# Strassen products in eight of the 22 blocks of an up projection, with their activation sums formed during the output projection

## The chip, the cores and the metric

The kernel runs on one core of one Trainium2 chip. The metric is the device time of an execution in microseconds (us), taken from launch to end on that core. The engines are named as in the profile: PE (matmul) and PEld (its weight load), DVE, ACT, POOL, and SP, which issues the DMAs.

## The reference

Two layers of an encoder trunk on 512 tokens with 1024 features, in float32. In each layer an input projection feeds three branches (latent attention, grouped-query attention, mean pooling), which are gated, merged and sent through an output projection. Then comes the gated feed-forward block, which is where the change lies:

```python
x = x + merged @ w_out[l]
hf = rms_norm(x, ffn_norm_g[l])
u = depthwise_conv(hf @ ffn_w_up[l], ffn_conv_w[l], ffn_conv_b[l])   # 1024 -> 2 * 2816, width 3
u_gate, u_val = u[..., :D_FF], u[..., D_FF:]
x = x + (jax.nn.silu(u_gate) * u_val) @ ffn_w_down[l]                # 2816 -> 1024
```

## The kernel before

**Layout.** Features lie on the 128 partitions and tokens along the free axis. `XM` holds the residual stream as 8 tiles of 128x512. `HH` and `HL` hold the same, scaled by the norm's gains, split in two: a rounded part (high) and the rest (low), both in the fp32r type that PE multiplies. The norm's factor for each token (`rbc`) is applied only when a product leaves PSUM. Every float32 product is three fp32r matmuls: high by high, high by low, low by high (`mm3`, L477, which calls `mm`; all its matmuls show as L470).

**Weights.** They come as a stream of pieces in the order of use. SP loads two pieces at a time into one of three `raw` buffers (`w_dma`). `w_split` (L377) turns a piece of 128x512 into a high part `wh` on ACT and a low part `wl` on POOL, or on DVE where the planner finds it sooner free. `wnext` keeps a few pieces ready ahead of PE.

**Up projection.** The 22 blocks of 128 gate features and the 22 of values are made in two halves, blocks 0 to 11 and 12 to 21 (`HALVES`). A block `c` has part 0 (gate) and part 1 (value). Each part is one PSUM bank filled by 24 matmuls of 512 columns (`feat_major`, L696: 8 tiles of features by three). `up_evac` (L1732) then empties the bank: DVE multiplies by `rbc`, ACT applies the middle tap and the bias, DVE adds the other two taps, ACT takes the silu of the gate, and DVE multiplies gate and value. For an odd block DVE also forms the sums of activations that the down projection wants, in a PSUM bank `q`.

**Down projection.** It already goes by Strassen's scheme. A piece holds a 2x2 group of 128x128 weight blocks, and the activations of a pair of blocks, cut in two halves of 256 tokens, are the other 2x2 group. `products` (L1807) makes seven products instead of eight, each of three matmuls of 256 columns (L1832), into four banks. `w_seven` (L400) prepares the seven left factors: three are blocks of the piece and four are sums. So a piece costs more work beside PE: ACT copies one block into a PSUM bank (`mi` or `S`, in turn), DVE forms the sums there in three instructions of 256, 128 and 128 columns, ACT writes their high part, DVE their low part (128x512), and the plain blocks are split as before (128x384). `unite` (L1836) adds the four banks to two tiles of `XM` on DVE, with the last two additions on POOL. Six PSUM banks (`acc`, `ST`, `AV`, two each) serve the up and the down projection.

**What sets the order.** All engines run what was written for them, in order. The program decides that order while it is built: a planner (`Clock`) keeps an imagined time with a cost for each instruction, and `chain` writes an instruction when its predecessors are done on that imagined time. The planner has no part in the execution; only the order that it wrote is left.

## Time and profile before

| | |
|---|---|
| median of 3 runs | 1551.59 us (1550.44 to 1551.61) |
| the profiled execution | 1551.91 us, of it 1550.1 us of span |
| granted clock | 0.999 |
| PE busy, matmuls | 1531.9 us, 7760 |
| PEld, DVE, ACT, POOL busy | 1307.6, 1090.8, 870.7, 1031.7 us |
| DMA | 166.63 MB, 107 GB/s |

The stages of the feed-forward block, read from PE's instructions by their tiles:

| stage | layer 0, us | layer 1, us |
|---|---|---|
| output projection | 379.0 to 422.8 | 1147.6 to 1191.4 |
| up, blocks 0 to 11 (and part 0 of 12) | 422.8 to 559.0 | 1191.4 to 1327.5 |
| down, first half | 559.0 to 621.3 | 1327.5 to 1389.9 |
| up, rest | 621.3 to 724.7 | 1389.9 to 1493.3 |
| down, second half | 724.7 to 776.0 | 1493.3 to 1544.6 |

A matmul's own duration in the trace overlaps with the next one's, so PE's cost is read from the starts: time of a stretch divided by the matmuls in it. A row of a view that groups instructions names line, engine, operation, tiles written and read, shape and count, then busy time, mean duration in ns, and the idle time before with what ended it.

### The profile page before, as it was taken

Reading aid. Unit: us, or ns where it says so; the run is one execution under the profiler, and the core shown is the slowest. Engines: PE = TensorE matmul, PEld = TensorE weight load, DVE = VectorE, ACT = ScalarE, POOL = GpSimd, SP = SyncE. Lnnn points to the kernel's source line nnn. Section 1 sums busy time; section 2 is a strip of 40 time slices with the busy share of each in tenths; the row PEclk is TensorE's granted clock in tenths of the full one; section 3 lists DMA queues with packets and bytes.
Section 4 is the critical chain, followed back from the end, with each engine's and each line's share of the span. In section 5 each row is a group of like instructions: output and inputs, shape, how many; then the busy total and the mean of one; then the engine's idle time right before and its main releaser. Section 6 shows DMA issues by size and latency. Waiting matters only on the chain.

```text
span 1550.1 us, 22862 instructions
## 1 busy us (share of the span) xinstructions
PE 1531.9 (99%) x7760; PEld 1307.6 (84%) x7760; DVE 1090.8 (70%) x1986; ACT 870.7 (56%) x1695; POOL 1031.7 (67%) x983
## 2 busy tenths in 40 slices
PE   9999999999999999999999999999999999999998
PEld 8888788788888889888988877888888888998888
DVE  6778889986255576557956788899762655765586
ACT  6557786663444455445644587776634455544453
POOL 4965986854666645665789659878547666465654
PEclk9999999999999999999999999999999999999999
DMA  6432234434333333333445322444243233233223
GB/s 217 114 113 77 75 102 133 124 91 141 104 95 97 95 91 106 106 98 91 132 126 138 105 70 75 117 139 125 82 147 99 96 96 95 90 116 96 95 90 101
DMA packets 82725, 166.63 MB, mean 107 GB/s; under 512 B 20912, under 2 KB 42672, under 8 KB 82608
## 3 DMA queue, kind: packets, MB, share of 16 engines
q1 hardware_dynamic: 82464, 165.16, 34.7%
q8 instruction: 61, 1.00, 0.3%
q14 instruction: 56, 0.46, 0.1%
q10 hardware_dynamic: 144, 0.01, 0.0%
HBM read 151.50 MB, written 13.63 MB: 107 GB/s over the span
## 4 chain that ended last, share of the span: by engine, by line
PE 87%; DVE 5%; ACT 3%; POOL 3%; issue 1%; DVEq 0%; POOLq 0%; ACTq 0%
PE ps_acc L470 34%; PE ps_AV L470 19%; PE ps_ST L470 15%; PE ps_AV L1832 5%; PE ps_ST L1832 5%; PE ps_acc L1832 4%; PE ps_S L470 2%; PE ps_mi L470 2%; PE ps_ST L1430 1%; POOL qa L272 1%; DVE XM L272 1%; ACT ps_ST L264 1%; DVE mgl L272 1%; POOL oraw L272 0%; ACT wh L264 0%
## 5 line engine op out<-in xcount | busy, mean ns | idle before, releaser
L272 POOL TENSOR_TENSOR wl<-raw,wh 128x512 fp32r<-128x512 f32 (+3 forms) x498 | 608.6, 1229 | 403.6 <-ACT wh L264 378.2
L264 ACT ACTIVATE wh<-raw 128x512 fp32r<-128x512 f32 (+2 forms) x521 | 300.9, 590 | 31.4 <-DMA raw<-w 12.0
L470 PE MATMUL ps_acc<-HH,wh 128*128 128x512 f32 x608 | 237.2, 390 | 0.2
L470 PE MATMUL ps_acc<-HL,wh 128*128 128x512 f32 x608 | 236.9, 390 | 0.0
L470 PE MATMUL ps_acc<-HH,wl 128*128 128x512 f32 x608 | 236.8, 389 | 0.0
L470 PEld LDWEIGHTS ps_acc<-HH,wh 128*128 128x128 f32 x608 | 114.2, 188 | 24.2 <-issue 0.8
L470 PEld LDWEIGHTS ps_acc<-HH,wl 128*128 128x128 f32 x608 | 114.2, 188 | 24.0
L470 PEld LDWEIGHTS ps_acc<-HL,wh 128*128 128x128 f32 x608 | 114.2, 188 | 23.2
L470 PE MATMUL ps_AV<-HH,wh 128*128 128x512 f32 x288 | 112.4, 390 | 0.0
L470 PE MATMUL ps_AV<-HL,wh 128*128 128x512 f32 x288 | 112.1, 389 | 0.0
L470 PE MATMUL ps_AV<-HH,wl 128*128 128x512 f32 x288 | 112.1, 389 | 0.0
L470 PE MATMUL ps_ST<-HH,wh 128*128 128x512 f32 x224 | 87.3, 390 | 0.0
L470 PE MATMUL ps_ST<-HL,wh 128*128 128x512 f32 x224 | 87.2, 389 | 0.0
L470 PE MATMUL ps_ST<-HH,wl 128*128 128x512 f32 x224 | 87.1, 389 | 0.0
L470 PEld LDWEIGHTS ps_AV<-HH,wl 128*128 128x128 f32 x288 | 54.1, 188 | 11.4
L470 PEld LDWEIGHTS ps_AV<-HH,wh 128*128 128x128 f32 x288 | 54.1, 188 | 11.0
L470 PEld LDWEIGHTS ps_AV<-HL,wh 128*128 128x128 f32 x288 | 54.1, 188 | 10.9
L276 DVE SCALAR_TENSOR_TENSOR a<-ps_acc,prm,a 128x511 f32<-128x511 f32 x64 | 47.9, 748 | 21.4 <-ACT a L264 20.5
L1832 PE MATMUL ps_ST<-ah,wh 128*128 128x256 f32 x278 | 55.5, 284 | 2.3 <-ACT wh L264 2.3
L276 DVE SCALAR_TENSOR_TENSOR a<-ps_AV,prm,a 128x511 f32<-128x511 f32 x56 | 42.0, 749 | 21.3 <-ACT a L264 20.3
L276 DVE SCALAR_TENSOR_TENSOR a<-ps_ST,prm,a 128x511 f32<-128x511 f32 x56 | 41.9, 749 | 20.0 <-ACT a L264 19.2
L264 ACT ACTIVATE gt<-gt 128x512 f32<-128x512 f32 x48 | 30.2, 628 | 45.3 <-DVE gt L272 45.1
(479 smaller groups left out, 4328.9 us busy)
## 6 DMA issues: line engine op xcount, KB each, us to landing
raw<-w SPq DMA_DIRECT2D x228, 512.0 KB, 3.5
raw<-w SPq DMA_DIRECT2D x13, 384.0 KB, 3.1
XM<-x SPq DMA_DIRECT2D x16, 256.0 KB, 3.4
dtq<-tr SPq DMA_DIRECT2D x16, 192.0 KB, 1.9
dtk<-tr SPq DMA_DIRECT2D x16, 192.0 KB, 2.0
tf<-dtq SPq DMA_DIRECT2D x48, 64.0 KB, 2.1
tf<-dtk SPq DMA_DIRECT2D x48, 64.0 KB, 2.1
raw<-w SPq DMA_DIRECT2D x6, 448.0 KB, 3.4
```

The lines of the kernel that those rows point to most:

```text
L264: return self.eng.activation(out, in_, func, **k)
L272: return self.eng.tensor_tensor(out, *a)
L276: return self.eng.scalar_tensor_tensor(out, *a)
L470: PE.matmul(o, lhsT=lhsT, rhs=rhs, start=start, stop=stop)
L1430: PE.matmul(sc, lhsT=s[a_][:, kb_], rhs=s[b_][:, :T], start=False, stop=n == len(pairs) - 1, skip_group_check=True)
L1832: PE.matmul(o, lhsT=x_, rhs=y_, start=first and b not in seen and q == 0, stop=False, skip_group_check=True)
```

## The change

1. **Blocks 2, 4, 6, 8, 10, 16, 18 and 20** of the up projection are made by `both`: the piece is a 2x2 group of weight blocks (two tiles of features by gate and value of block `c`), and `products` makes seven products for each of the four pairs of feature tiles. 96 matmuls of 512 columns become 84 of 256 columns for each pair of parts. Their 32 pieces per layer go through `w_seven` instead of `w_split`.
2. **The other factor**, the sums of activations (`turned`, tiles `tf`), is formed by `turn_pair` during the output projection, as soon as two tiles of `XM` are complete, in the banks `mi` and `S`; a copy goes to DRAM (`tsp`). The second half loads it back at block 13 (`load_turned`) and splits it again on ACT and POOL, since its 16 tiles are freed between.
3. **Four banks come out of such a block.** DVE adds them to two (five instructions), and those go through `up_evac`.
4. **`products`** takes the plain weight blocks first (2, 1, 4), then the sums' high parts, then their low parts; the old order stays for the pieces marked `late`.
5. **`unite`** puts its last addition on DVE instead of POOL. The very last `unite` has an order of its own with two additions on POOL and one copy on ACT.
6. **Smaller**: banks are taken from whichever tag is free soonest (`bank`) instead of in turn; the bank `q` is taken only when the product is written; the splits of block 11 go to POOL instead of DVE; the second norm of a layer leaves out `tokens` (two DVE instructions) and starts 0.8 after its sum instead of 2.0 in planner time; the first banks of layer 1 are chosen by `bank`.

```diff
+UP_SEVEN = (2, 4, 6, 8, 10, 16, 18, 20)
-    r = [(c, part) for c in range(c0, c1) for part in range(2)]
+    r = [z for c in range(c0, c1) for z in (((c, BOTH),) if c in UP_SEVEN else ((c, 0), (c, 1)))]
...
+        def turn_pair(k):
...
+            return [([("H", G2, k), ("H", G2, k + 1)], begin),
+                    stt(1, lo_, x1, hi_, g1, 0, lo_, ALU.subtract), stt(1, hi_, x2, hi_, g2, 1, lo_, ALU.add), hi(0),
+                    stt(0, lo_, x2, hi_, g2, 0, hi_, ALU.add), stt(0, hi_, x2, lo_, g2, 1, hi_, ALU.subtract), hi(1),
+                    lo(0), keep(0), lambda: free("S"), lo(1), keep(1), lambda: free("mi")]
...
-                eng = V if c + 1 in (HALVES[0][1], HALVES[1][1]) else G
+                eng = V if c + 1 == FC else G
...
-            for n in (2, 1, 3, 6, 5, 4, 7):
+            work = [(n, q) for n in ((2, 1, 3, 6, 5, 4, 7) if late else (2, 1, 4)) for q in range(3)]
+            if not late:
+                work += [(n, q) for n in (3, 6, 5, 7) for q in range(2)] + [(n, 2) for n in (3, 6, 5, 7)]
...
+        def both(c, half):
+            banks_ = {}
+            for k in range(0, KC, 2):
+                t = turned[k]
+                need(("H", G2, k), ("H", G2, k + 1))
+                products(((HH[:, k, :256], HL[:, k, :256]), (HH[:, k + 1, :], HL[:, k + 1, :]), t[:2], t[2:], ("H", G2, k),
+                          ("H", G2, k + 1), ("turned", l, half, k, 0), ("turned", l, half, k, 1)), banks_, k == 0)
...
+            chain(lambda: A.activation(u[:, :256], b1[:, :256], AF.Copy), after=0.0)
+            chain(add(u[:, hi_], u[:, :256], b1[:, hi_]), lambda: free(t1),
+                  add(v[:, :256], u[:, hi_], b3[:, :256]), lambda: free(t3),
+                  add(u[:, hi_], u[:, hi_], b2[:, hi_]), add(b0, u[:, :T], b0), lambda: up_evac(c, 0, b0, t0),
+                  add(pair(b2), bc(v[:, None, :256], [P, 2, 256]), pair(b2)), lambda: up_evac(c, 1, b2, t2), after=0.0)
...
-                  lambda: e.tensor_tensor(pair(x1), pair(x1), u3[:, None, :].to_broadcast([P, 2, 256]), ALU.add),
+                  lambda: V.tensor_tensor(pair(x1), pair(x1), u3[:, None, :].to_broadcast([P, 2, 256]), ALU.add),
```

**What moves on PE.** The first rows are those of block 2 in layer 0 before: HH and HL are the activations, wh and wl the weights' parts, ps_ST a bank.

```order
L470 MATMUL ps_ST_4911<-HH,wh_4843 128x512
L470 MATMUL ps_ST_4911<-HL,wh_4843 128x512
L470 MATMUL ps_ST_4911<-HH,wl_4844 128x512
L470 MATMUL ps_ST_4911<-HH,wh_4843 128x512
L470 MATMUL ps_ST_4911<-HL,wh_4843 128x512
```

The same place in the changed kernel is the end of the first seven products of block 2; wh_0 and wl_0 are the plain blocks of the piece, wh_1 and wl_1 the sums, tf the activation sums.

```order
L1895 MATMUL ps_acc_4927<-tf_4417,wl_0_4816 128x256
L1895 MATMUL ps_acc_4916<-HH,wh_1_4815 128x256
L1895 MATMUL ps_acc_4916<-HL,wh_1_4815 128x256
L1895 MATMUL ps_ST_4921<-tf_4415,wh_1_4815 128x256
L1895 MATMUL ps_ST_4921<-tf_4416,wh_1_4815 128x256
L1895 MATMUL ps_acc_4927<-tf_4415,wh_1_4815 128x256
L1895 MATMUL ps_acc_4927<-tf_4416,wh_1_4815 128x256
L1895 MATMUL ps_AV_4941<-tf_4417,wh_1_4815 128x256
L1895 MATMUL ps_AV_4941<-tf_4418,wh_1_4815 128x256
L1895 MATMUL ps_acc_4916<-HH,wl_1_4817 128x256
L1895 MATMUL ps_ST_4921<-tf_4415,wl_1_4817 128x256
```

One bank filled by matmuls of 512 columns has become four that are filled in turn by matmuls of 256; the low part of the sums (wl_1) is the last thing that a piece needs.

**What moves on DVE in the up projection.** Before, in layer 0 at blocks 3 and 4, DVE only empties banks (rbc, the two taps on a) and forms the sums of activations (t, sMQ).

```order
L272 TENSOR_TENSOR ps_AV_4956<-ps_AV_4956,rbc_4709 128x512
L276 SCALAR_TENSOR_TENSOR a_4996<-ps_AV_4956,prm_88,a_4996 128x511 x2
L272 TENSOR_TENSOR ps_acc_4997<-a_4996,a_4955 128x512
L272 TENSOR_TENSOR t_739_4998<-ps_acc_4997,t_739_4998 128x256
L272 TENSOR_TENSOR t_740_4999<-ps_acc_4997,a_4910 128x256
L272 TENSOR_TENSOR t_740_4999<-ps_acc_4997,t_739_4998 128x256
L272 TENSOR_TENSOR sMQ_4632<-ps_acc_4997,sMQ_4633 128x512
L272 TENSOR_TENSOR ps_ST_5002<-ps_ST_5002,rbc_4709 128x512
L276 SCALAR_TENSOR_TENSOR a_5051<-ps_ST_5002,prm_88,a_5051 128x511 x2
```

In the changed kernel this is where block 2 ends on DVE: u adds up the four banks, and ps_S with raw is the first weight piece of block 4.

```order
L276 TENSOR_TENSOR u_766_5061<-u_766_5061,ps_ST_4921 128x256
L276 TENSOR_TENSOR u_767_5062<-u_766_5061,ps_AV_4941 128x256
L276 TENSOR_TENSOR ps_S_4852<-ps_S_4852,raw_4975 128x256
L276 TENSOR_TENSOR u_766_5061<-u_766_5061,ps_acc_4927 128x256
L276 TENSOR_TENSOR ps_S_4852<-raw_4975,ps_S_4852 128x128
L276 TENSOR_TENSOR ps_acc_4916<-u_766_5061,ps_acc_4916 128x512
L276 TENSOR_TENSOR ps_S_4852<-raw_4975,ps_S_4852 128x128
L276 TENSOR_TENSOR ps_acc_4927<-u_767_5062,ps_acc_4927 128x512
L276 TENSOR_TENSOR ps_acc_4916<-ps_acc_4916,rbc_4784 128x512
L276 TENSOR_TENSOR wl_1_5069<-ps_S_4852,wh_1_5067 128x512
```

Ahead of the emptying of a bank stand now five additions and the four instructions of a weight piece, written in turn; the first addition waits for PE's last product of the block, and all rows behind it wait with it.

**What moves on DVE in the output projection.** Before, each tile of XM gets its residual and its low part, one after the other.

```order
L276 SCALAR_TENSOR_TENSOR XM<-ps_AV_4386,XM 128x512
L276 SCALAR_TENSOR_TENSOR HL<-XM,prm_88,HH 128x512
L276 SCALAR_TENSOR_TENSOR XM<-ps_acc_4427,XM 128x512
L276 SCALAR_TENSOR_TENSOR HL<-XM,prm_88,HH 128x512
L276 SCALAR_TENSOR_TENSOR XM<-ps_ST_4468,XM 128x512
```

Now the sums of tiles 0 and 1 stand between them: four instructions of 256 columns in the banks S and mi, and two low parts tf.

```order
L280 SCALAR_TENSOR_TENSOR ps_S_4420<-XM,prm_89,ps_mi_4419 128x256
L280 SCALAR_TENSOR_TENSOR ps_S_4420<-XM,prm_89,ps_S_4420 128x256
L280 SCALAR_TENSOR_TENSOR ps_mi_4419<-XM,prm_89,ps_mi_4419 128x256
L280 SCALAR_TENSOR_TENSOR XM<-ps_AV_4387,XM 128x512
L280 SCALAR_TENSOR_TENSOR ps_mi_4419<-XM,prm_89,ps_S_4420 128x256
L280 SCALAR_TENSOR_TENSOR HL<-XM,prm_89,HH 128x512
L276 TENSOR_TENSOR tf_4416<-ps_S_4420,tf_4415 128x512
L276 TENSOR_TENSOR tf_4418<-ps_mi_4419,tf_4417 128x512
```

## The prediction on record

> **What bounds the kernel now.** I start with the page: each engine's share, then the chain of work that ended last.
>
> ```profile
> PE 1531.9 (99%) x7760; PEld 1307.6 (84%) x7760; DVE 1090.8 (70%) x1986; ACT 870.7 (56%) x1695; POOL 1031.7 (67%) x983
> ...
> PE 87%; DVE 5%; ACT 3%; POOL 3%; issue 1%; DVEq 0%; POOLq 0%; ACTq 0%
> ```
>
> PE is busy 99% and carries 87% of the chain, so a matmul less is time less, as long as the others keep up. The next view is the busy time by stretch, for those that the change touches (columns: stretch, length, then busy time and count of PE, PEld, DVE, ACT, POOL).
>
> ```profile
> core 0: us, PE busy (x) PEld busy (x) DVE busy (x) ACT busy (x) POOL busy (x), PEclk, DMA share, GB/s
> 379.00:422.80 43.80, 43.80 (x193) 36.28 (x194) 14.72 (x19) 18.83 (x33) 28.53 (x24) 1.00 0.40 117
> 422.80:559.00 136.20, 136.20 (x604) 112.80 (x604) 79.35 (x121) 66.68 (x113) 86.94 (x73) 1.00 0.32 96
> 740.00:770.00 30.00, 30.00 (x252) 30.00 (x252) 28.26 (x67) 20.96 (x49) 23.98 (x21) 1.00 0.40 122
> 724.70:776.00 51.30, 50.72 (x422) 50.52 (x421) 46.82 (x105) 33.73 (x76) 33.19 (x31) 1.00 0.41 125
> ```
>
> In the up projection (422.8 to 559) PE never waits and DVE is idle 42% of the time. In the second down projection DVE is busy 28.26 of 30.00 us, and PE still 30.00 of 30.00.
>
> **Part 1, the products.** In the chain, parts of the up projection follow each other on PE; below are the first and the last of 21 in a row.
>
> ```profile
> 433.90 5.44 PE ps_AV L470 x24
> ...
> 542.70 5.44 PE ps_acc L470 x24
> ```
>
> Twenty parts of 24 matmuls take 108.80 us, so a matmul of 512 columns costs 226.7 ns. For 256 columns the starts in the down projection give the price:
>
> ```profile
> 732.64 0.28 PE L1832 MATMUL ps_acc<-al,wh 128*128 128x256 f32 x1
> 732.76 0.28 PE L1832 MATMUL ps_acc<-ah,wl 128*128 128x256 f32 x1
> 732.88 0.40 PE L1832 MATMUL ps_AV<-ah,wh 128*128 128x256 f32 x2
> 733.86 0.38 PE L1832 MATMUL ps_AV<-ah,wl 128*128 128x256 f32 x1 [0.58 <-DVE wl L272]
> ```
>
> They start 0.12 us apart (252 in the 30.00 us above say the same). Eight blocks in two layers lose 16 x 48 = 768 matmuls of 512 columns (174.1 us) and gain 16 x 84 = 1344 of 256 (161.3 us): **-12.8 us**, 0.8 per block. The gain is small, since a short matmul costs more than half a long one.
>
> The Trainium skill speaks against this step: "TensorE: Matmul & The Clock Gate", section "Back-to-back issue gap", gives a sustained spacing of about 81 ns at 128 columns and 131 ns at 512, since weight loads share the spacing. My estimate from that page is 98 ns at 256, and so 768 x 131 against 1344 x 98 ns: +31 us instead of -12.8. The trace disagrees on both numbers (226.7 and 120), and the sum goes by the trace.
>
> **Part 2, stalls that the new order may take away.** PE's few waits in and after the down projections, from its timeline:
>
> ```profile
> 565.92 0.50 PE L1832 MATMUL ps_ST<-ah,wh 128*128 128x256 f32 x2 [1.15 <-ACT wh L264]
> 566.65 0.39 PE L1832 MATMUL ps_ST<-ah,wl 128*128 128x256 f32 x1 [0.22 <-DVE wl L272]
> ...
> 777.22 0.44 PE L470 MATMUL ps_acc<-wh,HH 128*128 128x384 f32 x1 [0.71 <-DVE u L272]
> ...
> 1334.51 0.50 PE L1832 MATMUL ps_ST<-ah,wh 128*128 128x256 f32 x2 [1.15 <-ACT wh L264]
> ...
> 1502.46 0.39 PE L1832 MATMUL ps_AV<-ah,wl 128*128 128x256 f32 x1 [0.58 <-DVE wl L272]
> ```
>
> All wait for a piece's sums, but the one at 777. The new order of products asks for the sums' high part at the 10th matmul instead of the 7th (0.36 us later) and for the low part at the 18th instead of the 9th (1.08 us). The 0.58 should go, and of 1.37 (1.15 and 0.22) about half. Block 11's splits leave DVE, which helps; what is late next is the same piece's high part. I take -1.3 per layer, bounds 0 and -1.95. The wait at 777 is for a bank; layer 1 now begins with `mi`: -0.5, bounds 0 and -0.71. The end's reordered additions I take at 0 (bounds 0 and -1.3, two additions in this row):
>
> ```profile
> 1545.57 1.28 DVE L272 TENSOR_TENSOR XM<-XM,u 128x512 f32<-128x512 f32 x2
> ```
>
> Together -3.1.
>
> **Part 3, DVE in the changed blocks.** A Strassen block and the odd block behind it take PE 84 x 0.12 + 48 x 0.2267 = 20.96 us. What DVE owes in that time is priced by the groups by form.
>
> ```profile
> L272 DVE TENSOR_TENSOR wl<-ps_mi,wh 128x512 fp32r<-128x512 f32 x44 | 30.3, 688 | 17.5 <-ACT wh L264 15.3 <-PE ps_ST L1832 1.4 <-ACT HH L264 0.7
> L272 DVE TENSOR_TENSOR ps_mi<-raw,ps_mi 128x128 f32<-128x128 f32 x88 | 25.7, 292 | 1.9
> L272 DVE TENSOR_TENSOR ps_mi<-ps_mi,raw 128x256 f32<-128x256 f32 x44 | 18.6, 423 | 0.0
> L272 DVE TENSOR_TENSOR u<-u,ps_acc 128x256 f32<-128x256 f32 x10 | 4.1, 409 | 0.1
> L272 DVE TENSOR_TENSOR ps_acc<-ps_acc,rbc 128x512 f32<-128x512 f32 x32 | 22.3, 696 | 30.3 <-PE ps_acc L470 30.2
> L276 DVE SCALAR_TENSOR_TENSOR a<-ps_acc,prm,a 128x511 f32<-128x511 f32 x64 | 47.9, 748 | 21.4 <-ACT a L264 20.5
> L272 DVE TENSOR_TENSOR a<-a,a 128x512 f32<-128x512 f32 x22 | 18.1, 824 | 1.9 <-ACT a L264 1.2
> L272 DVE TENSOR_TENSOR t<-ps_acc,t 128x256 f32<-128x256 f32 x12 | 5.1, 425 | 5.8 <-ACT ah L264 3.4 <-ACT sMQ L264 1.7
> L272 DVE TENSOR_TENSOR ah<-ps_acc,ah 128x512 fp32r<-128x512 f32 x4 | 2.7, 680 | 0.0
> L272 DVE TENSOR_TENSOR XM<-XM,gt 128x512 f32<-128x512 f32 x16 | 18.5, 1157 | 0.3
> ...
> L264 ACT ACTIVATE u<-ps_acc 128x256 f32<-128x256 f32 x6 | 2.3, 381 | 5.1 <-PE ps_acc L1832 5.1
> ```
>
> Four weight pieces: 4 x (0.688 + 0.423 + 2 x 0.292) = 6.8. Five additions: 3 x 0.409 + 2 x 0.696 = 2.6. Emptying four parts: 4 x 0.696 + 8 x 0.748 = 8.8. Gate by value: 2 x 0.824 = 1.6. Activation sums: 3 x 0.425 + 0.680 = 2.0. In all **21.8 us in 39 instructions, for 20.96 of PE**. But durations overlap when instructions are independent, as these starts show:
>
> ```profile
> 752.55 0.68 DVE L272 TENSOR_TENSOR XM<-XM,ps_AV 128x512 f32<-128x512 f32 x1
> 753.15 0.29 DVE L272 TENSOR_TENSOR ps_S<-raw,ps_S 128x128 f32<-128x128 f32 x1
> 753.35 0.43 DVE L272 TENSOR_TENSOR ps_mi<-ps_mi,raw 128x256 f32<-128x256 f32 x1
> 753.68 0.41 DVE L272 TENSOR_TENSOR u<-u,ps_acc 128x256 f32<-128x256 f32 x1
> ```
>
> Each costs about 0.085 less than its duration: 39 x 0.085 = 3.3, so 18.5 at best. To it comes a wait that the order forces: the additions stand behind the low part of the block's last piece and wait until PE has used it (four matmuls, 0.48, and one duration, 0.28) and ACT has copied a bank (0.38): 1.1 us in which DVE has little to do. In all a pair takes DVE 19.6 to 22.9 us, against 20.96: PE waits between 0 and 2.0 us per pair, 0 to 32 for 16 pairs. The nearest stretch is 740 to 770, whose groups on DVE begin and end so:
>
> ```profile
> L276 DVE SCALAR_TENSOR_TENSOR HL<-XM,prm,HH 128x512 fp32r<-128x512 f32 x5 | 5.7, 1140 | 0.0
> ...
> L272 DVE TENSOR_TENSOR u<-u,ps_acc 128x256 f32<-128x256 f32 x1 | 0.4, 405 | 0.0
> ```
>
> Its 13 groups sum to 32.9 us in 30.00, a density of 1.10 with no wait of PE; a new pair has 21.8 in 20.96, 1.04. So I take the lower part of the range, 0.25 per pair: **+4.0**.
>
> **Part 4, the rest.** `unite`'s last addition moves to DVE, four times per down projection at up to 1.157 us. In layer 0's second half this meets 46.82 busy of 51.30, which just fills it: +1.0, bounds 0 and +4.6; elsewhere DVE has room. The Trainium skill, "SBUF — State Buffer", section "Who interferes with whom", says that a DVE instruction with two SBUF inputs contends with a POOL instruction that reads SBUF. The rows agree (XM<-XM,gt 1157 ns, with an operand in PSUM 696); by it this addition costs 1.157 and not 0.696.
>
> The activation sums of one pair of tiles cost DVE four instructions of 256 columns (estimate 0.425 each, as the t row) and two low parts, 3.1 us, and ACT five copies at some 0.6, 3.0 us, four times per layer beside 14.72 of 43.80 and 18.83 of 43.80 busy in the output projection. The last pair follows tile 7's low part, and its two banks are wanted by the weights of block 2 after the third part:
>
> ```profile
> 424.30 0.75 DVE L276 SCALAR_TENSOR_TENSOR HL<-XM,prm,HH 128x512 fp32r<-128x512 f32 x1 [0.79 <-ACT HH L264]
> ...
> L264 ACT ACTIVATE wh<-ps_mi 128x512 fp32r<-128x512 f32 x44 | 26.3, 597 | 40.4 <-DVE ps_mi L272 28.3 <-PE ps_acc L1832 5.3 <-PE ps_ST L1832 4.9
> ```
>
> From 425.1 it has until 439.1 (422.8 and three parts), 14 us for 6.1 in series: hidden, cost 0. Were that cover gone, each us late would stop PE as long, once per layer. SP's queue gets 8 stores and 8 loads of 256 KB per layer among the weight loads; such loads land soon:
>
> ```profile
> XM<-xsp SPq DMA_DIRECT2D x8, 256.0 KB, 2.7
> ```
>
> Block 13 loads them and block 16 wants them, six parts (33 us) later; POOL pays 8 more splits there and saves a quarter of its work on 32 pieces. Cost 0, up to +2 if weight loads behind them come late.
>
> **The sum:** -12.8 - 3.1 + 4.0 + 1.0 = -10.9 against the profiled execution's 1551.9 (the runs' median is 0.3 lower): **1541.0 us**.
>
> **Rivals.** *DVE takes half the gain back* (18 in 100 for this and worse short of a loss): pairs wait 0.8 us instead of 0.25, 16 x 0.55 = +8.8, 1549.8. For it: the in-order wait and 1.04. Against: 740 to 770. *DVE becomes the bound* (8 in 100): dependent instructions and collisions with POOL leave no overlap, a pair takes 22.9, PE waits 2.0; 16 x 1.75 = +28, 1569. It turns slower than before from 0.93 us per pair on. *All stalls vanish and DVE keeps up* (15 in 100): -12.8 - 4.6 - 1.3 = 1533.2. *Weight loads set the spacing* (1 in 100): each new matmul would cost its weight load's own duration.
>
> ```profile
> L1832 PEld LDWEIGHTS ps_ST<-ah,wh 128*128 128x128 f32 x278 | 43.8, 192 | 2.7 <-ACT wh L264 2.7
> ```
>
> That is 1344 x 0.192 - 161.3 = +97, 1638; the break-even is 129.5 ns, and the down projection holds 120 with such loads, hidden behind the matmul before. It is the mechanism of the spacing rule named in part 1.
>
> My forecast has 58 in 100. The range 1533 to 1551 leaves out the slow cases and little else. A measurement of this kernel can tell about 0.2% (3.1 us) from no change; faster than 1548.5: 0.81, within: 0.09, slower: 0.10.
>
> **What would show it.** Right: 1344 more matmuls of 256 columns at 120 ns; DVE about 95% busy in blocks 2 to 11 with waits of PE under 0.5 us at each Strassen block; no 0.58 in the second down projections. Wrong: waits of PE for wl, wh or a bank of 1 us or more at every Strassen block, or for tf at block 2 or 16, or idle DVE with PE waiting, which would say that the order and not the load is at fault.

## The result and the profile after

The changed kernel takes 1541.18 us (median of 4 runs, 1540.13 to 1541.95), against 1551.60 (1550.44 to 1551.65) before: a ratio of 0.9934, 95% interval 0.9917 to 0.9951. Its profiled execution took 1541.37 us, 1539.3 of it span. The forecast was 1541.0. The total came out, but terms of the sum were wrong by 0.6 to 2.5 us, in both directions.

The page's first and fourth part, as read before:

```profile
PE 1520.7 (99%) x8336; PEld 1324.1 (86%) x8336; DVE 1221.3 (79%) x2379; ACT 946.8 (62%) x1896; POOL 1030.9 (67%) x986
...
PE 83%; DVE 7%; ACT 4%; POOL 3%; issue 2%; DMA 1%; SPq 0%; POOLq 0%; DVEq 0%; ACTq 0%
```

PE is still busy 99%, now in 576 more and shorter matmuls; DVE has 130 us more to do, and its share of the chain has gone from 5 to 7%. The busy time by stretch, each stretch reaching from a stage's first matmul to the next stage's (output projection, up, down, up, down of layer 0, then the first up stage of layer 1):

```profile
378.38:421.99 43.61, 43.60 (x192) 36.12 (x193) 23.65 (x37) 27.07 (x48) 28.11 (x23) 1.00 0.47 146
421.99:554.34 132.35, 132.35 (x783) 118.18 (x782) 111.99 (x230) 82.71 (x163) 83.21 (x74) 1.00 0.34 106
554.34:615.85 61.51, 60.73 (x505) 60.52 (x504) 45.82 (x113) 33.28 (x79) 33.91 (x31) 1.00 0.34 104
615.85:716.90 101.05, 101.05 (x566) 88.79 (x565) 81.09 (x157) 60.16 (x118) 68.75 (x59) 1.00 0.38 120
716.90:768.85 51.95, 51.13 (x421) 50.55 (x420) 46.27 (x110) 35.30 (x81) 35.44 (x32) 1.00 0.41 129
1184.35:1317.67 133.32, 133.32 (x784) 118.54 (x783) 112.28 (x230) 83.14 (x163) 83.23 (x74) 1.00 0.33 105
```

The table gives the same lengths for every kernel of this study, worked out from the starts of PE's matmuls (us; "tail" reaches from the start of PE's last matmul to the end; the second four stages are those of layer 1). The attention part between the layers is left out: it took 371.0 to 372.4 us in the changed kernel and the twelve runs below, 371.76 before and 371.86 after, and the start up to the output projection 377.3 to 379.0. A difference of less than 1 us between two totals can be this alone, so the stages decide.

| kernel | up 1 | down 1 | up 2 | down 2 | up 1, layer 1 | down 1, layer 1 | up 2, layer 1 | down 2, layer 1 | tail | median |
|---|---|---|---|---|---|---|---|---|---|---|
| before | 136.25 | 62.37 | 103.39 | 51.22 | 136.25 | 62.37 | 103.39 | 51.11 | 5.81 | 1551.60 |
| after | 132.35 | 61.51 | 101.05 | 51.95 | 133.31 | 61.55 | 101.30 | 52.27 | 6.50 | 1541.18 |
| order_old | 133.34 | 60.69 | 101.60 | 51.39 | 134.43 | 60.70 | 102.47 | 51.44 | 6.68 | 1541.42 |
| order_mix | 132.35 | 61.16 | 101.05 | 51.97 | 133.97 | 61.17 | 101.28 | 52.35 | 6.50 | 1540.04 |
| xm_first | 132.35 | 60.71 | 101.05 | 51.85 | 133.43 | 60.97 | 101.35 | 52.51 | 5.81 | 1539.34 |
| poolx | 132.35 | 62.65 | 101.05 | 52.58 | 133.15 | 62.67 | 101.32 | 52.37 | 6.50 | 1544.19 |
| split | 132.35 | 60.80 | 101.05 | 52.10 | 133.91 | 60.83 | 101.97 | 52.60 | 5.81 | 1540.36 |
| split_v11 | 132.35 | 62.49 | 101.05 | 52.10 | 133.29 | 63.95 | 101.35 | 52.41 | 5.81 | 1543.46 |
| no_seven | 136.25 | 61.56 | 103.39 | 51.46 | 136.25 | 61.56 | 103.39 | 51.34 | 6.50 | 1550.06 |
| dummy | 135.27 | 62.48 | 102.51 | 52.61 | 135.24 | 62.28 | 102.49 | 52.51 | 6.51 | 1551.48 |
| with3 | 135.83 | 61.53 | 101.05 | 51.96 | 137.57 | 61.56 | 101.26 | 52.45 | 6.49 | 1549.10 |
| tail | 132.35 | 61.53 | 101.05 | 51.95 | 133.43 | 61.54 | 101.13 | 52.40 | 5.81 | 1540.44 |
| xm_g21 | 132.35 | 60.71 | 101.07 | 50.77 | 132.89 | 60.73 | 101.59 | 51.27 | 5.81 | 1537.14 |
| xm14g | 132.35 | 60.69 | 102.15 | 50.77 | 133.14 | 60.69 | 102.22 | 51.31 | 5.87 | 1537.41 |

Before to after, the up stages get shorter by 3.90 + 2.34 + 2.94 + 2.09 = 11.3 us. The down stages get longer by 0.2 in all (the first are 0.8 shorter each, the second 0.7 and 1.2 longer), the tail by 0.7. The output projection stays at 43.6, with 23.65 us of work on DVE in it instead of 14.72, and 27.07 on ACT instead of 18.83.

In the down projections PE now waits in other places. Its timeline, rows with a wait in the first 20 us of layer 0's two halves (idle time and releaser in brackets):

```profile
571.12 0.39 PE L1895 MATMUL ps_acc<-sMQ,wh 128*128 128x256 f32 x1 [0.78 <-DVE XM L276]
...
727.00 0.38 PE L1895 MATMUL ps_ST<-ah,wl 128*128 128x256 f32 x1 [0.35 <-DVE wl L276]
731.43 0.51 PE L1895 MATMUL ps_ST<-sMQ,wh 128*128 128x256 f32 x2 [0.46 <-DVE XM L276]
```

The waits of before, for sums at a group's start, are gone from the first halves; in the second halves one for a low part is still there (the row at 727.00). New ones stand at the second pair of tiles, for a bank that DVE's addition to XM sets free. (Matmul ends are modelled, so the bracket understates; between the starts 0.94 and 0.61 us are lost at 571 and 731.) They come in every down projection: 0.94, 0.98, 0.61 and 0.61, 3.1 us in all. What DVE did ahead of the first:

```profile
568.40 0.63 DVE L276 TENSOR_TENSOR ps_mi<-raw,ps_mi 128x128 f32<-128x128 f32 x2
569.78 0.69 DVE L276 TENSOR_TENSOR wl<-ps_mi,wh 128x512 fp32r<-128x512 f32 x1 [0.75 <-ACT wh L268]
570.38 0.68 DVE L276 TENSOR_TENSOR XM<-XM,ps_acc 128x512 f32<-128x512 f32 x1
```

DVE stood idle for 0.75 us, waiting for ACT's `wh`, with the addition that PE needed written behind that instruction.

In the up projection, DVE over one Strassen block and the ordinary block behind it (20.96 us, layer 0): the stretch, and then the three rows with a wait of 0.4 us or more.

```profile
512.00:532.96 20.96, 20.96 (x135) 19.07 (x134) 18.49 (x40) 13.43 (x28) 13.18 (x12) 1.00 0.33 101
```

```profile
514.58 0.42 DVE L276 TENSOR_TENSOR t<-ps_AV,t 128x256 f32<-128x256 f32 x1 [0.66 <-ACT ah L268]
...
517.39 0.42 DVE L276 TENSOR_TENSOR u<-u,ps_acc 128x256 f32<-128x256 f32 x1 [1.19 <-ACT u L268]
...
529.42 0.69 DVE L276 TENSOR_TENSOR wl<-ps_mi,wh 128x512 fp32r<-128x512 f32 x1 [0.44 <-ACT wh L268]
```

DVE is busy 18.49 us of it, and PE never waits. Layer 1 has the same work (112.28 against 111.99 us) and takes 1 us more in up 1; there the last three pairs of blocks take 21.3 us each instead of 20.98 (from the starts), since four matmuls of a block's last piece come 0.04 to 0.11 us late.

### The profile page after: what moved, and what is told of

It is laid out like the page before. It is cut to its first block, busy times and chain, and to the rows that moved or that the text cites. A ratio compares the mean times of both kernels' runs of the same rounds, so it can differ in the third digit from the quotient of the medians.

```text
span 1539.3 us, 24815 instructions
## 1 busy us (share of the span) xinstructions
PE 1520.7 (99%) x8336; PEld 1324.1 (86%) x8336; DVE 1221.3 (79%) x2379; ACT 946.8 (62%) x1896; POOL 1030.9 (67%) x986
## 4 chain that ended last, share of the span: by engine, by line
PE 83%; DVE 7%; ACT 4%; POOL 3%; issue 2%; DMA 1%; SPq 0%; POOLq 0%; DVEq 0%; ACTq 0%
PE ps_acc L488 23%; PE ps_AV L488 17%; PE ps_ST L488 13%; PE ps_acc L1895 10%; PE ps_AV L1895 7%; PE ps_ST L1895 6%; PE ps_S L488 2%; PE ps_mi L488 2%; POOL qa L276 1%; DVE XM L276 1%; POOL oraw L276 1%; ACT wh L268 1%; DVE vt L280 1%; DVE pl L276 1%; PE ps_ST L1450 1%
## 5 line engine op out<-in xcount | busy, mean ns | idle before, releaser
L268 ACT ACTIVATE wh<-raw 128x512 fp32r<-128x512 f32 (+2 forms) x521 | 292.8, 578 | 20.1 <-PE ps_ST L488 10.3
L488 PE MATMUL ps_acc<-HH,wh 128*128 128x512 f32 x416 | 162.8, 391 | 0.0
L488 PE MATMUL ps_acc<-HL,wh 128*128 128x512 f32 x416 | 162.3, 390 | 0.0
L488 PE MATMUL ps_acc<-HH,wl 128*128 128x512 f32 x416 | 162.1, 390 | 0.0
L488 PEld LDWEIGHTS ps_acc<-HH,wl 128*128 128x128 f32 x416 | 78.1, 188 | 16.5
L488 PEld LDWEIGHTS ps_acc<-HH,wh 128*128 128x128 f32 x416 | 78.1, 188 | 16.2 <-DVE gt L276 0.6
L268 ACT ACTIVATE wh<-ps_S 128x512 fp32r<-128x512 f32 x76 | 45.2, 594 | 54.9 <-DVE ps_S L276 45.2
L268 ACT ACTIVATE wh<-ps_mi 128x512 fp32r<-128x512 f32 x76 | 45.2, 595 | 49.5 <-DVE ps_mi L276 43.9
L276 DVE TENSOR_TENSOR wl<-ps_S,wh 128x512 fp32r<-128x512 f32 x76 | 52.1, 685 | 14.8 <-ACT wh L268 13.1
L276 DVE TENSOR_TENSOR wl<-ps_mi,wh 128x512 fp32r<-128x512 f32 x76 | 52.1, 686 | 13.4 <-ACT wh L268 11.7
L1895 PE MATMUL ps_AV<-ah,wh 128*128 128x256 f32 x304 | 60.5, 283 | 0.0
```

What stands on the lines that cost most here:

```text
L268: return self.eng.activation(out, in_, func, **k)
L276: return self.eng.tensor_tensor(out, *a)
L488: PE.matmul(o, lhsT=lhsT, rhs=rhs, start=start, stop=stop)
L1895: PE.matmul(banks_[b][1][:, 256 * at_:256 * at_ + 256], lhsT=(his, his, los)[q][i][:, ws], rhs=right[n][q == 1], start=first and b not in ...
```

## The experiments

Each kernel is the changed one with the edit shown. None leaves out a part of the computation; `dummy` adds an instruction whose output is not used.

**The order of the products, put back everywhere (order_old).**

```diff
-            work = [(n, q) for n in ((2, 1, 3, 6, 5, 4, 7) if late else (2, 1, 4)) for q in range(3)]
-            if not late:
+            work = [(n, q) for n in (2, 1, 3, 6, 5, 4, 7) for q in range(3)]
+            if False:
```

> The changed kernel with the old order of the seven products (2, 1, 3, 6, 5, 4, 7, three matmuls each) everywhere. Two theories on the waits of 0.95 to 1.15 us that the changed kernel shows in every down projection at the second pair of tiles. Theory A, the order makes them: the new order finishes the first bank 3 matmuls before a group's end (old: 12) and asks for the third at the 7th matmul of the next group (old: 16th). Then all four waits (4.0 us together) go with the old order, and the prediction's part 2 comes back in its place: about 1.4 us at the start of each first down projection, 0.4 to 0.6 per second one, and new waits for a piece's sums in the Strassen blocks of the up projection, where DVE is fullest (0 to 0.5 per block). Net within -2 to +8 of the changed kernel: 1539 to 1549. Theory B, DVE is simply fuller there and any order waits: the waits stay at 0.9 or more each, and the time rises by 2 us or more.

Measured 1541.42 us (ratio to before 0.9935, 0.9920 to 0.9949). The busy time by stretch of layer 0's first up and down stage, and one wait of PE in layer 1's up projection:

```profile
422.08:555.42 133.34, 133.34 (x784) 118.46 (x783) 112.12 (x230) 83.89 (x163) 83.19 (x74) 1.00 0.32 105
555.42:616.11 60.69, 60.69 (x506) 60.53 (x504) 47.33 (x114) 34.34 (x80) 34.47 (x31) 1.00 0.33 105
```

```profile
1236.63 0.38 PE L1895 MATMUL ps_ST<-HH,wl 128*128 128x256 f32 x1 [0.57 <-DVE wl L276]
```

Theory A: the four waits go. The first down stages run at 60.7, without a wait of PE over 0.03, neither the new one nor the one of before; so the stall at their start in the kernel before was not the old order's doing alone. In the second halves the old order has a wait of its own, 0.91 and 1.07 us between the starts, for a piece's low part. (By the lists in `products`, the old order asks for the third bank at the 13th matmul, not at the 16th.) The up stages get longer by 0.99 + 0.55 + 1.12 + 1.17 = 3.8. So, with the old order put back in both at once, the new order is worth 3.8 us in the up projection and costs 3.1 in the down projection.

**The third bank asked for 0.48 us later (order_mix).**

```diff
+            if first and not late:
+                work = [(n, q) for n in (2, 1) for q in range(3)] + [(n, q) for n in (3, 6) for q in range(2)]
+                work += [(4, q) for q in range(3)] + [(n, q) for n in (5, 7) for q in range(2)] + [(n, 2) for n in (3, 6, 5, 7)]
```

> The changed kernel, but in the first piece of each group of products the order is 2 and 1 whole, the high parts of 3 and 6, then 4, then 5 and 7, and the low parts of 3, 6, 5 and 7 last, so that the third bank is asked for at the 11th matmul and not at the 7th (0.48 us later). Theory A (the order makes the waits at the second pair of tiles): each of the four shrinks by 0.48, 1.9 us together, and since the high part of the sums is asked for 3 matmuls earlier, up to 0.36 of wait may come in its place at a group's start; 1539 to 1541, read from the trace more than from the time. Theory B (DVE's load alone): the four waits stay at 0.9 to 1.1 us each.

Measured 1540.04. By the starts the wait for the third bank at the second pair of tiles fell by about 0.48 in all four places, as theory A had it: from 0.94 and 0.98 to 0.48 in the first halves, from 0.61 to 0.13 in the second. But in the second halves PE then waits 0.65 instead of 0.17 for the bank behind it, which DVE's `u` sets free. So the first down stages get shorter by 0.35 to 0.38, the second ones do not, and layer 1's first up stage gets 0.7 longer. So when the bank is asked for is one half of the matter; the other is when DVE frees it.

**DVE's addition ahead of the next low part (xm_first).** A call at the last matmul of the first bank writes the addition; the tail is that of before the change (below).

```diff
                 seen.add(b)
+                if hook and (n, q) == (3, 2):
+                    hook(banks_[0])
...
-            chain(add(x0, x0, b0), lambda: free(t0), add(u2, p1, b1[:, hi_]), lambda: free(t1),
+            chain(add(u2, p1, b1[:, hi_]), lambda: free(t1),
...
+                def first_bank(z, m=m):
+                    chain(lambda: V.tensor_tensor(XM[:, m, :], XM[:, m, :], z[1], ALU.add), lambda: free(z[0]), after=0.0)
...
```

> The changed kernel, new order of products kept, but the addition that frees the first bank of a pair of tiles (XM plus the first bank) is written as soon as that bank's last product is written, and not after the last matmul of the pair; the tail as before the change. So DVE meets it ahead of the next piece's low part, for which it waits 0.75 us. Theory A (what DVE has in front of it makes the four waits of 0.94 to 0.98 and 0.61 to 0.66 at the second pair of tiles, together 3.1): they shrink to 0 to 0.3 each, 1541.2 - 0.7 - 2.0 to 3.1 = 1537.4 to 1538.5. Theory B (the third bank is asked for too soon in the new order, whatever DVE has in front): at least 0.6 of each 0.95 stays and the time is 1540 to 1540.5.

Measured 1539.34 (0.9925, 0.9908 to 0.9941). DVE at the second pair of tiles in layer 0's first half, and PE at the same place:

```profile
568.44 0.68 DVE L276 TENSOR_TENSOR XM<-XM,ps_acc 128x512 f32<-128x512 f32 x1
569.04 0.29 DVE L276 TENSOR_TENSOR ps_mi<-raw,ps_mi 128x128 f32<-128x128 f32 x1
570.08 0.69 DVE L276 TENSOR_TENSOR wl<-ps_mi,wh 128x512 fp32r<-128x512 f32 x1 [0.74 <-ACT wh L268]
```

```profile
569.99 0.40 PE L1895 MATMUL ps_acc<-sMQ,wh 128*128 128x256 f32 x2
```

DVE waits for ACT as long as before (0.74), but the addition now stands ahead of that wait, and PE does not wait. With the products' order kept, all four waits fell to 0.08 or less. Theory A; the expected 2.0 to 3.1 came only in part (0.8 and 0.6 in the first halves, 0.1 and -0.2 in the second), since the second halves wait at a later pair instead (0.60 and 0.85 us between the starts, again for DVE's XM).

**unite's last addition back on POOL (poolx).**

```diff
-                  lambda: V.tensor_tensor(pair(x1), pair(x1), u3[:, None, :].to_broadcast([P, 2, 256]), ALU.add),
+                  lambda: G.tensor_tensor(pair(x1), pair(x1), u3[:, None, :].to_broadcast([P, 2, 256]), ALU.add),
```

> The changed kernel with the last addition of each pair of tiles in the down projections back on POOL, as before. The prediction priced its place on DVE at +1.0 us, in layer 0's second down projection. Theory A (that price): 1.0 less, that stage 51.0 instead of 51.95 us. Theory B (DVE has room, the stage's waits come from the order of the products): all stages within 0.3 us, and POOL's later end may cost up to 1 us at the end of the kernel or at the start of layer 1; 1540.5 to 1542.5.

Measured 1544.19 (0.9952, 0.9937 to 0.9967): 3 us slower than the changed kernel, outside both expectations. The first down stages take 1.1 us more, in two waits of 0.47 at the third and fourth pair of tiles. DVE at the third pair in this kernel, and PE:

```profile
586.09 0.69 DVE L276 TENSOR_TENSOR wl<-ps_mi,wh 128x512 fp32r<-128x512 f32 x1 [0.74 <-ACT wh L268]
586.70 0.68 DVE L276 TENSOR_TENSOR XM<-XM,ps_AV 128x512 f32<-128x512 f32 x1
```

```profile
587.43 0.51 PE L1895 MATMUL ps_AV<-sMQ,wh 128*128 128x256 f32 x2 [0.32 <-DVE XM L276]
```

And the same place in the changed kernel:

```profile
585.45 0.69 DVE L276 TENSOR_TENSOR XM<-XM,ps_AV 128x512 f32<-128x512 f32 x1 [0.89 <-PE ps_AV L1895]
586.06 0.68 DVE L276 TENSOR_TENSOR wl<-ps_mi,wh 128x512 fp32r<-128x512 f32 x1
```

With one instruction less on DVE, the planner wrote `wl` ahead of the addition, and the wait of the second pair appears at the third and fourth as well. What the addition itself costs is 0.84 us of DVE on average, by the group in the changed kernel:

```profile
L276 DVE TENSOR_TENSOR XM<-XM,u 128x512 f32<-128x512 f32 x16 | 13.5, 843 | 0.1
```

Where it was moved changed the order around it, and that was worth more than its duration.

**New order for the up projection, old for the down projection (split).** The tail too is that of before the change.

```diff
-                    products(right_of(k // 2), banks_, k == c0, m == 0 and k == c1 - 2 or l == L - 1 and m == KC - 2 and k == FC - 2)
+                    products(right_of(k // 2), banks_, k == c0, True)
```

> The changed kernel with the new order of products in the Strassen blocks of the up projection only, the old order everywhere in the down projections, and the very last additions as before the change (one of 512 columns back on DVE). Theory A (the new order is worth about 3.8 us in the up projections and costs about 3.1 in the down projections; the special tail costs 0.7; the three add up): 1541.2 - 3.1 - 0.7 = 1537.4, with up stages as in the changed kernel within 0.3 and down stages 60.7 and 51.4 us. Theory B (what the down stages gain comes back in the next stage, since DVE owes the same work): 1540 to 1541.5.

Measured 1540.36 (0.9927, 0.9912 to 0.9942). The first down stages get 0.7 shorter each, as A has it. The second ones get longer by 0.2 and 0.3, and layer 1's up stages by 0.6 and 0.7, which is B: of the 3.1 us that the new order costs in the down stages, 1.0 comes back when it is taken out of them alone. At the start of the second halves the old order meets DVE late:

```profile
726.32 0.39 PE L1895 MATMUL ps_ST<-ah,wl 128*128 128x256 f32 x1 [1.12 <-DVE wl L276]
```

**Block 11's splits back on DVE (split_v11).** Against the run before.

```diff
-                eng = V if c + 1 == FC else G
+                eng = V if c + 1 in (HALVES[0][1], FC) else G
```

> As the run before (new order in the up projection alone, the tail as before), with block 11's splits back on DVE. It asks what took away the stall of 1.31 and 0.38 at the start of each first down projection, which the prediction put down to the new order. Theory A (moving block 11's splits to POOL did it): the stall returns in both layers, 1.2 to 1.7 each, so 2.4 to 3.4 us above the run before. Theory B (the order did it, or the addition of unite that moved to DVE): the splits alone bring back less than 0.4 per layer, under 0.8 in all.

Measured 1543.46, 3.1 above the run before; the first down stages take 62.49 and 63.95. PE at their start in layer 0, and DVE just ahead of it:

```profile
561.89 0.50 PE L1895 MATMUL ps_acc<-ah,wh 128*128 128x256 f32 x2 [1.27 <-ACT wh L268]
562.62 0.39 PE L1895 MATMUL ps_acc<-ah,wl 128*128 128x256 f32 x1 [0.22 <-DVE wl L276]
```

```profile
555.97 0.68 DVE L276 TENSOR_TENSOR ah<-t,ah 128x512 fp32r<-128x512 f32 x1
...
557.77 0.42 DVE L276 TENSOR_TENSOR ps_S<-ps_S,raw 128x256 f32<-128x256 f32 x1
558.10 0.68 DVE L276 TENSOR_TENSOR ah<-t,ah 128x512 fp32r<-128x512 f32 x1
```

This is the stall of before, with both its parts. Theory A: the two splits `ah<-t,ah` on DVE, with the order that follows from them, make it, and moving them to POOL takes it away. (A third, `ah<-ps_AV,ah`, is on DVE in both kernels.) That holds with the old order in the down projection; no run has the new order there and these splits on DVE.

In layer 1 the stage grew by 3.1 us, but only 1.7 of it is this stall, as in layer 0. The rest is the clock granted to PE (the third number from the end of the row) just behind it:

```profile
1327.40:1330.80 3.40, 3.40 (x19) 3.40 (x18) 1.92 (x6) 1.74 (x5) 1.59 (x2) 0.51 0.15 58
```

For 3.4 us the granted clock is 0.51, and 16 matmuls of 256 columns start 0.21 us apart instead of 0.12, 1.4 us in all. Neither layer 0 of this run nor the kernel before, with stalls about as long, shows such a drop; why it came here is open. So that the total of 3.1 lies where theory A put it is partly chance: the clock's 1.4 us is in it, and layer 1's up stages came out 0.6 us shorter each than in the run before.

**No Strassen block in the up projection (no_seven).**

```diff
-UP_SEVEN = (2, 4, 6, 8, 10, 16, 18, 20)
+UP_SEVEN = ()
...
-        turn_features()
...
-                if c0 and c == c0 + 1 and part != 1:
+                if UP_SEVEN and c0 and c == c0 + 1 and part != 1:
```

> The changed kernel with no block of the up projection by Strassen's scheme and without the sums of activations: all else of the change stays (order of products in the down projections, unite, banks, block 11's splits, norm). Theory A (the products are worth 12.8 less some 1.5 of waits): the up stages go back to 136.2 and 103.4 us, 11.3 more in all: 1552.5. Theory B (the rest of the change carries part of the gain, as the prediction's part 2 has it with -3.1): 1549 to 1551, with down stages clearly under those of before.

Measured 1550.06 (0.9990, 0.9981 to 1.0000). Layer 0's first up and second down stage:

```profile
421.53:557.78 136.25, 136.25 (x603) 112.84 (x602) 77.14 (x119) 66.65 (x113) 87.16 (x73) 1.00 0.31 96
...
722.73:774.19 51.46, 50.64 (x422) 50.44 (x421) 45.52 (x107) 33.85 (x76) 33.30 (x30) 1.00 0.40 130
```

The up stages are those of before, to 0.01 us: the whole 11.3 us there is the Strassen blocks'. The second down stages are 0.5 and 0.9 shorter than with the blocks: the waits for a piece's sums in their first 11 us (0.51 in layer 0, 0.29 and 0.57 in layer 1) are absent. The waits at the second pair of tiles are there without any Strassen block too, 0.98 to 1.00 us at each of the four places, so the blocks' load on DVE is not what makes them. The rest of the change is worth about 1.5 us (its interval reaches from 2.9 to 0). By the stages it is -1.6 in the first down stages, +0.5 in the second, +0.7 in the tail; what is left of the difference lies in the start and the attention, which vary by as much. Theory A for the up stages; theory B's total, but not for its reason.

**One more instruction on DVE per Strassen block (dummy).**

```diff
-            u, v = slot("u2"), slot("u3")
+            u, v, extra = slot("u2"), slot("u3"), slot("ex")
...
-                  add(v[:, :256], u[:, hi_], b3[:, :256]), lambda: free(t3),
+                  add(v[:, :256], u[:, hi_], b3[:, :256]), lambda: free(t3), add(extra[:, :T], u[:, :T], b0),
```

> The changed kernel with one more addition of 512 columns on DVE in each of the 16 Strassen blocks, between the two additions that free banks; its output is used by nothing (the computation itself is not changed). It reads a bank, so it costs 0.68 us of duration and 0.60 of spacing. Theory A, as the prediction's part 3 has it: DVE is at its limit in these blocks and each microsecond more stops PE: 16 x 0.6 = 9.6 more, 1550.8. Theory B, the changed kernel's trace (DVE busy 111.99 of 132.18 us in the first part of the up projection, waits of 0.1 per block at most in layer 0, 0.2 in layer 1): it falls into idle time. Layer 0's up stages stay within 0.3 of 132.35 and 101.05; layer 1's, where a piece's sums are already late by 0.05 to 0.1, gain at most 0.3 per block; 1541 to 1543.5.

Measured 1551.48 (0.9998, 0.9989 to 1.0008): 10.3 more, theory A's number. The mechanism is only half that of theory A. The same pair of blocks as above, which now takes 21.71 us, and in it DVE's multiplication of gate and value, and POOL:

```profile
517.37:539.08 21.71, 21.45 (x135) 19.18 (x133) 19.86 (x40) 13.09 (x28) 13.45 (x13) 1.00 0.31 98
```

```profile
535.82 1.54 DVE L276 TENSOR_TENSOR ps_ST<-a,a 128x512 f32<-128x512 f32 x1
```

```profile
534.52 3.98 POOL L276 TENSOR_TENSOR wl<-raw,wh 128x384 fp32r<-128x384 f32 x3 [0.96 <-ACT wh L268]
```

And the same multiplication in the changed kernel, with POOL:

```profile
532.56 0.69 DVE L276 TENSOR_TENSOR ps_ST<-a,a 128x512 f32<-128x512 f32 x1
```

```profile
532.96 2.68 POOL L276 TENSOR_TENSOR wl<-raw,wh 128x512 fp32r<-128x512 f32 x2 [0.59 <-ACT wh L268]
```

There POOL stood idle when the multiplication began; in `dummy` its splits were running.

DVE's busy time grew by 19.86 - 18.49 = 1.37: 0.60 for the instruction, and 0.77 because gate times value, shifted by it, now starts while POOL's weight splits run and takes 1.54 instead of 0.69. Of these 1.37, 0.62 went into DVE's idle time (2.47 before, 1.85 now), and 0.75 onto the pair. The multiplication takes 1.54 us in four of layer 0's six pairs up to block 11, and the four Strassen blocks behind them (4, 6, 8 and 10) lose 0.73 us each by the starts; block 2 loses nothing. So there was room for about 0.6 us per pair, and a small instruction that shifts another into a collision exceeds it. That 0.60 alone would have fitted is worked out, not run. Another 2.6 of the 10.1 us in the trace lie in the down stages, where the planner's order moved too (a wait of 1.91 instead of 0.94 at the second pair).

**Three Strassen blocks in a row (with3).**

```diff
-UP_SEVEN = (2, 4, 6, 8, 10, 16, 18, 20)
+UP_SEVEN = (2, 3, 4, 6, 8, 10, 16, 18, 20)
```

> The changed kernel with block 3 by Strassen's scheme too, so that blocks 2, 3 and 4 follow each other with no ordinary block between: 2 x 0.8 = 1.6 us less on PE by the prediction's prices. It asks for DVE's real cost of a Strassen block. By the prediction's rows such a block alone owes 6.8 + 2.6 for weights and additions, 4.4 for emptying, some 1.8 for gate and sums: about 15.6 of durations, 13.6 with the overlap, and the forced wait of 1.1, in 10.08 us of PE. Theory A (DVE sets the pace there): PE waits 3.5 to 5.5 us in the blocks 2 to 4 of each layer, net +2 to +4 per layer: 1545 to 1549. Theory B (the ordinary blocks 0 and 1 ahead and 5 behind give enough slack, since weights are prepared some pieces ahead): under 1.6 of waits per layer, 1539.5 to 1541.5.

Measured 1549.10 (0.9980, 0.9971 to 0.9989): theory A by its size. The stages of up 1 are 3.48 and 4.26 longer; with the 0.8 that the products save, 4.3 and 5.1 us more of waits per layer. By the starts, 3.0 us of that are lost in blocks 3 and 4 of each layer. The rest is lost later, in blocks 6 and 8 (in layer 1 also 10), where neither theory had it; why was not traced. The stretch around blocks 2 to 4, and PE in it:

```profile
444.00:474.00 30.00, 28.11 (x227) 27.40 (x226) 29.12 (x69) 20.30 (x45) 16.26 (x17) 1.00 0.29 87
```

```profile
466.89 0.50 PE L1895 MATMUL ps_ST<-tf,wh 128*128 128x256 f32 x2 [1.26 <-DVE u L276]
...
473.22 0.38 PE L1895 MATMUL ps_acc<-HH,wh 128*128 128x256 f32 x1 [0.63 <-ACT wh L268]
```

DVE is busy 29.12 of 30.00 us and PE only 28.11: here DVE is the bound. The prediction's second rival exists; alternate blocks are what keeps the change clear of it.

**The last additions as before (tail).**

```diff
-            if rush:
+            if False:
...
-                  add(x0, x0, u[:, :T], G), lambda: then and then(m),
+                  add(x0, x0, u[:, :T], V if rush else G), lambda: then and then(m),
```

> The changed kernel without the special order of its very last additions: one addition of 512 columns goes from POOL back to DVE, as before. Theory A, POOL's two additions in series (1.27 us each) and the store queued behind them make the end longer: from PE's last matmul to the end 5.8 us as before, not 6.5, so 0.7 us less, 1540.5. Theory B (the end is set by the stores' landing, whatever comes ahead of them): 6.5 as in the changed kernel, no difference.

Measured 1540.44; by the trace the tail is 5.81 instead of 6.50 us, theory A to 0.01 us. The end of the changed kernel, on POOL, DVE and the store queue:

```profile
1532.95 2.54 POOL L276 TENSOR_TENSOR XM<-XM,u 128x512 f32<-128x512 f32 x2 [5.44 <-DVE u L276]
...
1534.22 0.69 DVE L276 TENSOR_TENSOR XM<-XM,u 128x512 f32<-128x512 f32 x1
1535.52 0.81 SPq L1970 DMA_DIRECT2D out<-XM  x2
```

And with the additions as before:

```profile
1533.72 1.28 DVE L276 TENSOR_TENSOR XM<-XM,u 128x512 f32<-128x512 f32 x2
1534.43 0.93 SPq L1970 DMA_DIRECT2D out<-XM  x2
```

The two additions in series on POOL end at 1535.49, 0.58 after DVE's last, and both stores leave only then, the second queued behind the first though its tile was complete at 1534.91.

**Block 21's splits on POOL as well (xm_g21).** On top of xm_first.

```diff
-                eng = V if c + 1 == FC else G
+                eng = G
```

> As the run with the first bank's addition written early, and with the splits of the activations of block 21 on POOL instead of DVE. Theory A (the waits at the start of the second down projections, 0.52 and 0.95 us, come from DVE being taken by block 21's splits, as block 11's did to the first ones): they shrink to under 0.2 each, 1539.3 - 1.1 = 1538.2. Theory B (POOL is slower, and these splits are the last thing that the down projection's last pieces need or they collide with its weight splits): the waits move to another place of the same stage, which stays at 51.8 to 52.6.

Measured 1537.14 (1536.30 to 1537.54; 0.9905, 0.9890 to 0.9919), the fastest kernel here. Its second down stage of layer 0:

```profile
716.61:767.39 50.78, 50.68 (x422) 50.47 (x421) 44.99 (x108) 34.97 (x81) 35.38 (x33) 1.00 0.41 128
```

The second down stages are 1.1 and 1.2 us shorter than in xm_first; of the waits at their start 0.26 and 0.55 are left (expected under 0.2), and the wait at the later pair went too. So theory A, by its total; the kernel is about 4 us below the changed one, in the down stages and the tail.

**Block 14 too (xm14g).** On top of xm_g21.

```diff
-UP_SEVEN = (2, 4, 6, 8, 10, 16, 18, 20)
+UP_SEVEN = (2, 4, 6, 8, 10, 14, 16, 18, 20)
```

> As the run with the first bank's addition early and block 21's splits on POOL, with block 14 by Strassen's scheme too. It tries for more and asks how much room the loading back of the activation sums has, which the prediction put at nothing. By the changed kernel's trace POOL splits the loaded sums from 626.7 to 640.8 us (8 of 1.3 to 1.5 each), block 14 would start at 632.9 and want its four pairs at 633.6, 636.2, 638.7 and 641.2, which have theirs at 629.3, 634.9, 637.9 and 640.8: 0.4 to 1.3 us of room. Theory A (it fits): 0.8 per layer less, the second up stages 100.3 and 100.8, 1537.1 - 1.6 = 1535.5. Theory B (POOL's weight splits for block 14 stand behind the sums in its queue, or DVE is at its limit): PE waits 1 to 5 us at block 14 in each layer: 1537.5 to 1545.

Measured 1537.41 (1536.70 to 1537.75; 0.9908, 0.9891 to 0.9924), no gain: the second up stages are 1.08 and 0.63 longer instead of 0.8 shorter. POOL, DVE and PE in block 14 of layer 0:

```profile
623.63 10.76 POOL L276 TENSOR_TENSOR tf<-t,tf 128x512 fp32r<-128x512 f32 x8 [2.74 <-ACT tf L268]
...
636.07 4.07 POOL L276 TENSOR_TENSOR wl<-raw,wh 128x384 fp32r<-128x384 f32 x3
```

```profile
637.58 1.43 DVE L276 TENSOR_TENSOR ps_ST<-a,a 128x512 f32<-128x512 f32 x1
638.92 0.28 DVE L276 TENSOR_TENSOR ps_mi<-raw,ps_mi 128x128 f32<-128x128 f32 x1
```

```profile
639.97 0.39 PE L1895 MATMUL ps_acc<-HH,wh 128*128 128x256 f32 x1 [0.46 <-ACT wh L268]
```

The sums of activations were split in time (634.4, the block began at 631.0), but POOL was kept by them for 10.8 us, did its weight splits in one run afterwards, and that run made gate times value on DVE 1.43 us long; the piece's sums (`ps_mi`) stood behind it, ACT's `wh` behind those, and PE behind that. So in layer 0 theory B, in its first form, by way of DVE: 1.14 us are lost in block 14 and 0.73 in block 16. In layer 1 block 14 runs without a wait, and block 16 loses 1.23 us instead; how the one leads to the other was not traced.

## Why the prediction was right, and where it was not

**Part 1 held.** For each block 48 matmuls of 512 columns became 84 of 256, as the prediction has it (the list of the change says 96). The up stages of layer 0 got shorter by 3.90 and 2.34 us for five and three blocks, 0.78 per block against 0.80; no_seven shows that all of it is the blocks'. The 84 matmuls of 256 columns in such a block start 0.12 us apart, as in the down projection, and there was no wait for `tf` at block 2 or 16.

**Part 3 was mis-sized, too high by 2.5.** The up stages got shorter by 11.3 us of the 12.8, so waits and all else took 1.5, not 4.0. The lower end of the range was good: 18.5 us of work as worked out from the overlap (18.49 measured), and a forced wait of 1.1 (1.19). So DVE was busy 88% of a pair, not 95%. Missing was a second in-order wait, 0.66, for ACT's `ah` ahead of the last activation sum. Work and the two waits (1.85, as much idle time as is left in `dummy`) make 20.34 together, against 20.96 of PE. The step that failed is "0.25 per pair", a place within a range: as long as work and forced waits stay below PE's time, a pair waits 0, and layer 0 does so. Layer 1 lost 1.0 and 0.2 more, 0.28 to 0.36 in four of its eight pairs. Why the two layers differ with the same work is open.

**Part 2 failed, by 1.8 with part 4's down-projection term in it.** It put the first halves' stall down to the order of the products and took half of it off; but the old order runs without it (order_old), and block 11's splits bring it back (split_v11). So that stall went entirely, 1.69 us between the starts, and an edit that the text mentions only as a help is enough for it. Whether the new order alone would have taken half of it, no run shows. What the step missed is what the new order does at the other end: a bank is asked for at the 7th matmul of a pair of tiles, while DVE's freeing addition stands behind a low part that waits 0.75 us for ACT. Those 3.1 us, and the second halves' waits at the start, took the gain back: +0.2 for the four stages, where -2.6 and part 4's +1.0 stood. Of the second halves' 0.58, which should have gone, a wait of 0.35 for a low part is left in layer 0, and 0.41 in layer 1 with one of 0.13 ahead of it. The bank wait at layer 1's start (0.71) is gone as forecast, but the attention part is as long as before (371.86 against 371.76). The trace shows where the gain went: PE is 1.0 us ahead 17 us into this part and 1.2 us 236 us into it, and loses that behind, among other places in two waits of 0.42 and 0.45 us for DVE's `vt`, which the kernel before does not have. In no_seven and with3 such waits are absent, and the part takes 371.09 and 371.35; why they come is open.

**Part 4: +1.0 had the wrong sign.** The addition on DVE is 0.84 us on average, not 1.157, and putting it back on POOL makes the kernel 3 us slower, through the order that the planner then writes. The sums during the output projection cost nothing, as said (43.61 against 43.64). The tail, taken at 0 with bounds of 0 and -1.3, cost +0.69, outside its bounds: two additions in series on an engine that took 1.27 us for each.

**The sum** came out to 0.2 us by luck, since the errors cancel: 2.5 too much in part 3, against 1.8 in the down stages, 0.6 at layer 1's start and attention, and 0.7 in the tail that were not in it; another 0.6 less is the start up to the output projection, where the two kernels do the same. Of the rivals, DVE as the bound is real one step further on (with3, dummy), "all stalls vanish" is what xm_g21 comes nearest to (1537.1, against 1533.2), and the weight loads set no spacing.

## What to carry to other kernels

An engine that takes its work in order can set the pace while 9% idle (1.85 of 21.71 us in `dummy`), and with 12% idle it had only 0.6 us of room: count its forced waits into the cycle, and as a first guess take the wait of the engine it feeds as nothing until work and forced waits exceed the cycle (layer 1's 0.3 us per block shows that this is not exact). An instruction that frees a bank should not be written behind one that waits for a third engine; look for that at every place where the product order asks for a bank sooner. And where a planner writes the order, moving one instruction is an edit of the whole order: price it by the rows that result, not by its duration.

## What the runs showed of the hardware

The same DVE multiplication with both operands in SBUF took 0.69 us where it began with POOL idle, though one of POOL's splits began 0.40 us into it, and 1.43 to 1.54 us where it began while POOL's weight splits ran. That is a loss as large as a whole instruction, decided by a shift of 0.6 us. The Trainium skill, "SBUF — State Buffer", section "Who interferes with whom", names this pair of engines as one that contends; the trace agrees, and gives the size. The 0.085 us that independent DVE instructions overlap held in the changed kernel too (the rows at 569.78 and 570.38: starts 0.60 apart at 0.69 of duration).
